# Three products of split fp32 weights: one accumulator and three 256-column matmuls in place of two halves and a join

## The chip, the cores and the metric

The kernel runs on one core of a Trainium2 chip. The metric is the device time of one execution in microseconds (us). Three runs of the kernel before gave 2520.5, 2520.75 and 2521.31 us, median 2520.75.

## The reference

A causal decoder trunk of two layers works on one sequence of 256 tokens with 2048 features, all in fp32. Each layer is

```
a = rmsnorm(h, attn_norm[i])
h = h + mixer(a)                                  # layer 0: stick-breaking and dilated heads; layer 1: forgetting attention
h = h + conv_ffn(rmsnorm(h, ffn_norm[i]))         # up projection to 2 x 5632, causal convolution of width 3,
                                                  # silu(gate) * value, down projection
h = h + sigmoid(rmsnorm(h, ple_norm[i]) @ w_ple_gate[i]) * (p[i] @ w_ple[i])
```

and a last rmsnorm follows. Nearly all of the arithmetic is in the products of activations with weights: q, k and v (2048 x 6144), the output projection (2048 x 2048), the up projection (2048 x 11264), the down projection (5632 x 2048) and the gate (2048 x 2048).

## The kernel before

**Products.** Every weight w and every activation a is kept as a sum of two fp32r parts, w = w0 + w1 and a = a0 + a1, and a product is w0 a0 + w0 a1 + w1 a0. The activations stand feature-major, 128 features to a partition, in tiles `act` of shape 128 x 16 x 2 x 256: for each of the 16 tiles k of features the two parts lie side by side, 256 tokens each. Two such tiles (X and Y in the code) take turns as input and output of the stages.

**Weight stream.** All weights come in one stream of pieces, in the order of their use. A piece holds up to 4 tiles k of 256 columns. `issue_group` (line 149) has SyncE bring pieces in transfers of up to 1 MB. `split_unit` makes the parts of a piece: ScalarE casts (line 165), VectorE subtracts (line 166), into one of four tiles `w`. Pieces are split up to three ahead of their use (`LOOK = 3`).

**Two matmuls for three products.** `gemm_unit` takes a piece and, for each half j of its 256 columns and each tile k, issues two matmuls into a result `ps[:, j]` of 512 columns of the accumulator memory (PSUM):

```
nc.tensor.matmul(ps[:, j], lhsT=w[:, k, 0, js], rhs=a, ...)                # line 207, 512 columns: w0 a0 | w0 a1
nc.tensor.matmul(ps[:, j, 1, :], lhsT=w[:, k, 1, js], rhs=a[:, 0, :], ...) # line 209, 256 columns: w1 a0 onto w0 a1
```

The result thus stands in two halves whose sum is wanted. `gemm_v` (lines 242 and 244) does the same for v with the activations as the stationary operand. A matmul is two instructions: the weight load (PEld in the profile) and the matmul (PE). `flat=True` (line 203), used for the products psp of the layer's own inputs p alone, issues three matmuls of 256 columns into one half; so do `gemm_vf` (line 256, 272 columns, the first v of layer 1 with its forget gates) and the last pair of gates (line 734, pse and psg).

**Joins.** `joined` has ScalarE copy one half of a result out (line 263) and VectorE add the other (line 264); the next step, for example the multiplication by the norm's reciprocal root `rb` (line 634), reads the sum. It serves psq, psk, psu and psg. `add_to_h` does the like for pso and psd (lines 270 to 272), and the end of `head_pair` for psv (lines 623 and 624).

**Accumulators.** The results of the projections come from `mm_tile`: 2 buffers of 2 x 512 columns each. Everything else (norm sums nps, rows rps, scores scs and sps, attention outputs avp) comes from `at_tile`, also 2 buffers of that size, as does psp of layer 1.

**Order.** The code of a layer is written in the order of its stages: 8 pairs of heads, each with psq, psk and psv of 4 pieces; then the 8 pairs of outputs of pso; then three blocks of the feed-forward network, each with its psu pieces and then psd; then 8 pairs psg of gates. Work of TensorE that waits for other engines is put off by some pieces: `defer(n, fn)` runs fn after n more pieces have been issued. So the small matmuls of attention and of the norm (nps at line 306, rps at line 339) stand within the rows of the projections. A scheduler then orders each engine's instructions by when it expects their inputs, so that nps and rps can stand in the middle of a piece.

Of the kernel before, what the change touches and what calls it, by code (L numbers as in the profile page):

```python
# [17 lines left out]
P = 128  # L18
D = 2048
S = 256  # L20
# [40 lines left out]
def _units():  # L61
    """Pieces of the weights, in the order in which they are used."""
    full = _cuts(KT)
    ple = [[("w_ple", l, 0, 2, c * 256, 256) for c in range(8)] for l in range(DEPTH)]
    out = list(ple[0])
    for l in range(DEPTH):
        for hp in range(NH // 2):
            if l % 2 == 1 and hp == 0:
                out += [("w_vf", l, k0, kc, 2 * D, 256 + NH) for k0, kc in VF_CUTS]
            for part in range(3):  # L70
                if l % 2 == 0 or hp > 0 or part < 2:
                    out += _pair("w_in", l, part * D + hp * 256, 0, full)
# [12 lines left out]

def _groups(units):
    """Pieces that one transfer brings."""
    out, i = [], 0
    while i < len(units):
        room = 512 if i < 2 else 1024 if i < 12 else 2048  # L90
        n, size = 0, 0
        while i + n < len(units) and size + units[i + n][3] * units[i + n][5] <= room:
            size += units[i + n][3] * units[i + n][5]
            n += 1
        out.append(units[i:i + n])
        i += n
    return out
# [7 lines left out]
def trunk(ctx: ExitStack, tc: tile.TileContext, xT, pT, pos, gains, conv, bf, cst, wst, out):  # L105
# [22 lines left out]
    def mm_tile(name):  # L128
        return psum.tile([P, 2, 2, S], F32, name=name, tag="mm", bufs=2)
# [49 lines left out]
    # what waits for other engines is given to TensorE some pieces later  # L179
# [14 lines left out]
    def gemm_unit(ps, act, kind, l, c0, k0, first, last, koff=0, flat=False):  # L194
        """ps[:, j, 0] and ps[:, j, 1] sum to W[:, 128 columns]^T A^T."""
        kc, w = unit(kind, l, k0, c0)
        for j in range(2):
            js = slice(j * P, (j + 1) * P)
            for k in range(kc):
                a = act[:, k0 - koff + k]  # L200
                if flat:
                    for n, (s, t) in enumerate(((0, 0), (0, 1), (1, 0))):
                        nc.tensor.matmul(ps[:, j, 0, :], lhsT=w[:, k, s, js], rhs=a[:, t, :],  # L203
                                         start=first and k == 0 and n == 0,
                                         stop=last and k == kc - 1 and n == 2)
                    continue
                nc.tensor.matmul(ps[:, j], lhsT=w[:, k, 0, js], rhs=a,  # L207
                                 start=first and k == 0, stop=False, skip_group_check=True)
                nc.tensor.matmul(ps[:, j, 1, :], lhsT=w[:, k, 1, js], rhs=a[:, 0, :],  # L209
                                 start=False, stop=last and k == kc - 1, skip_group_check=True)  # L210
        tick()

    def gemm(ps, act, kind, l, c0, cuts, k0=0, koff=0, part=None, flat=False):
        n = len(cuts)
        for i, kc in enumerate(cuts):
            if part is None or i in part:
                gemm_unit(ps, act, kind, l, c0, k0, i == 0, i == n - 1, koff, flat)
            k0 += kc

    def staggered(name, act, kind, l, cuts, done, k0=0, koff=0):  # L220
        """All pairs of outputs; the first two end together."""
        n = len(cuts)
        ps = [mm_tile(name) for _ in range(2)]
        for part in (range(n - 1), (n - 1,)):
            for op in range(2):
                gemm(ps[op], act, kind, l, op * 256, cuts, k0, koff, part)
                if part == (n - 1,):
                    done(op, ps[op])
        for op in range(2, 8):
            p = mm_tile(name)  # L230
            gemm(p, act, kind, l, op * 256, cuts, k0, koff)
            done(op, p)

    def gemm_v(ps, act, l, c0):
        """ps[:, t, 0] and ps[:, t, 1] sum to A[tokens of tile t] W[:, 256 columns]."""
        for i in range(4):
            kc, w = unit("w_in", l, 4 * i, c0)
            for t in range(2):
                tsl = slice(t * P, (t + 1) * P)
                for k in range(kc):  # L240
                    a = act[:, 4 * i + k]
                    nc.tensor.matmul(ps[:, t], lhsT=a[:, 0, tsl], rhs=w[:, k],  # L242
                                     start=i == 0 and k == 0, stop=False, skip_group_check=True)
# [17 lines left out]
    def joined(ps):  # L261
        t = t2_tile("jn")
        nc.scalar.copy(out=t, in_=ps[:, :, 1, :])  # L263
        nc.vector.tensor_add(out=t, in0=t, in1=ps[:, :, 0, :])  # L264
# [15 lines left out]
    def norm_parts(op, g, dst):  # L280
        """h pair op is final: its parts, with the gains."""
# [17 lines left out]
    def norm_sums(more=()):  # L299
        """Reciprocal roots of the mean squares, one token a partition."""  # L300
# [23 lines left out]
    def norm_rows(mixer):  # L324
        """The same, one token a column, in every partition."""
# [23 lines left out]
    def with_rows(fn):  # L349
        """fn reads rb: not before norm_rows."""  # L350
# [14 lines left out]
    def ple_up(l, op):  # L365
        """A pair of p W_ple, kept until its gates are there."""
        ps = at_tile("psp").rearrange("p j (a s) -> p j a s", a=2) if l > 0 else mm_tile("psp")
        gemm(ps, pact, "w_ple", l, op * 256, (2,), flat=True)
        nc.scalar.copy(out=pl[:, 2 * op:2 * op + 2, :], in_=ps[:, :, 0, :])
# [150 lines left out]
    def sm_second(pe, s):  # L520
        """The weights, one key a partition."""
# [60 lines left out]
    def head_pair(l, hp, act, dst, st):  # L582
# [4 lines left out]
        if l % 2 == 1 and hp == 0:  # L587
            ps = mm_tile("psv").rearrange("p t a s -> p t (a s)")
# [7 lines left out]
        with_rows(lambda ps=ps: nc.vector.tensor_mul(out=q, in0=joined(ps), in1=rq2))  # L596
# [24 lines left out]
        t = t2_tile("jv")  # L621
        for i in range(2):
            nc.scalar.activation(out=t[:, i, :], in_=ps[:, i, 1, :], func=AF.Copy, scale=rT[:, i:i + 1])
            nc.vector.scalar_tensor_tensor(out=v[:, i, :], in0=ps[:, i, 0, :], scalar=rT[:, i:i + 1],
                                           in1=t[:, i, :], op0=ALU.mult, op1=ALU.add)

    def ffn_group(l, g, g0, act, hid):
        c = [t2_tile("yg"), t2_tile("yv")]

        def conv_taps(half, ps):  # L630
# [3 lines left out]
            nc.vector.tensor_mul(out=u[:, :, 2:], in0=joined(ps), in1=rb2)  # L634
# [19 lines left out]
    X, Y = bufs  # L654
    for l in range(DEPTH):
# [51 lines left out]
        for op in range(8):  # L707
            end = l + 1 == DEPTH and op == 7
            if end:
                ws = [unit("w_ple_gate", l, 4 * i, op * 256)[1] for i in range(4)]  # L710
                ps = [at_tile("pse"), mm_tile("psg")[:, 0]]
# [4 lines left out]
            def gate(op, ps, hs):  # L716
                gt = joined(ps)
                nc.vector.tensor_mul(out=gt, in0=gt, in1=rb2)
# [10 lines left out]
            else:  # L729
                more = []  # L730
                for j in range(2):
                    for k in range(KT):
                        for n, (a, b) in enumerate(((0, 0), (0, 1), (1, 0))):
                            nc.tensor.matmul(ps[j][:, 0, :S],
# [5 lines left out]
                    nc.vector.tensor_mul(out=gt, in0=ps[j][:, 0, :S], in1=rb)  # L740
# [95 lines left out]
```

## Time and profile before

| | |
|---|---|
| median of three runs | 2520.75 us |
| span of the profiled execution | 2519.2 us |
| TensorE matmuls | 14270, busy 2497.2 us |
| TensorE weight loads | 14270, busy 2173.1 us |
| VectorE | 2386 instructions, busy 1716.3 us |
| ScalarE | 1747 instructions, busy 1319.4 us |
| moved by DMA | 457.20 MB, 181 GB/s on average |
| granted TensorE clock | full in every slice of the span |

The profiled execution has a span of its own, 1.5 us below the median of the runs. A matmul starts before the one ahead of it has ended, and the ends are modelled, so its duration (397 ns for 512 columns, 281 ns for 256) is longer than the distance to the next start. In the timeline the first column is the start and the second the duration in us, from the first start to the last end where rows are merged (xN). PE is the matmul, PEld the weight load, DVE VectorE, ACT ScalarE. A name such as psu<-act,w gives the tile written and the tiles read.

### The profile page before, as it was taken

What the parts mean: (1) busy time and instruction counts of PE and PEld (TensorE: products, weight loads), DVE (VectorE), ACT (ScalarE), POOL (GpSimd) and SP (SyncE); (2) the same over time, 40 slices, a digit from 0 to 9 for tenths busy, and PEclk for the clock granted to TensorE, in tenths of its full rate; (3) what the DMA queues carried; (4) which work ended last, traced back from release to release, by engine and by line L of the source; (5) the groups of instructions that cost most, each with busy time, mean ns of one, the idle gap of its engine ahead of it and who ended that gap; (6) DMA issues with size and microseconds to landing.
All of it is one profiled execution on the core that took longest, in us unless ns stands there. A gap on an engine that the chain in (4) does not pass through costs nothing. (4 is left out here: it accounts for less than half of the span.)

```text
span 2519.2 us, 34810 instructions
## 1 busy us (share of the span) xinstructions
PE 2497.2 (99%) x14270; PEld 2173.1 (86%) x14270; DVE 1716.3 (68%) x2386; ACT 1319.4 (52%) x1747; POOL 2.5 (0%) x8
## 2 busy tenths in 40 slices
PE   8999999999999999999999999999999999999997
PEld 7888888888888888888888888888888888888887
DVE  7767667776567657777765555677765776677676
ACT  6554455554455445555554444555544554455564
POOL 0000000000000000000000000000000000000000
PEclk9999999999999999999999999999999999999999
DMA  7444455555555555555454444555555555555553
GB/s 259 167 168 167 167 184 184 185 184 192 183 193 184 180 188 184 190 181 199 170 179 163 163 161 165 183 192 184 187 184 184 187 184 186 193 187 180 182 191 117
DMA packets 66431, 457.20 MB, mean 181 GB/s; under 512 B 7408, under 2 KB 7424, under 8 KB 16608
## 3 DMA queue, kind: packets, MB, share of 16 engines
q1 hardware_dynamic: 66096, 454.53, 50.5%
q8 instruction: 111, 1.82, 0.3%
q0 software_dynamic: 176, 0.46, 0.1%
q14 instruction: 48, 0.39, 0.0%
HBM read 452.86 MB, written 2.10 MB: 181 GB/s over the span
## 5 line engine op out<-in xcount | busy, mean ns | idle before, releaser
L166 DVE TENSOR_TENSOR w<-wr,w 128x1024 fp32r<-128x1024 f32 (+2 forms) x882 | 1049.8, 1191 | 532.3 <-ACT w L165 529.9
L165 ACT CAST w<-wr 128x1024 fp32r<-128x1024 f32 (+2 forms) x882 | 903.4, 1025 | 710.6 <-PE psd L209 186.7
L207 PE MATMUL psu<-act,w 128*128 128x512 f32 x2816 | 995.5, 397 | 0.0
L209 PE MATMUL psu<-act,w 128*128 128x256 f32 x2816 | 791.3, 281 | 0.0
L207 PEld LDWEIGHTS psu<-act,w 128*128 128x128 f32 x2816 | 529.4, 188 | 130.6
L209 PEld LDWEIGHTS psu<-act,w 128*128 128x128 f32 x2816 | 528.6, 188 | 0.0
L207 PE MATMUL psd<-act,w 128*128 128x512 f32 x1408 | 497.8, 397 | 0.0
L209 PE MATMUL psd<-act,w 128*128 128x256 f32 x1408 | 395.6, 281 | 0.0
L207 PEld LDWEIGHTS psd<-act,w 128*128 128x128 f32 x1408 | 264.7, 188 | 65.3
L209 PEld LDWEIGHTS psd<-act,w 128*128 128x128 f32 x1408 | 264.3, 188 | 0.0
L207 PE MATMUL psq<-act,w 128*128 128x512 f32 x512 | 183.9, 400 | 0.0
L207 PE MATMUL psk<-act,w 128*128 128x512 f32 x512 | 182.8, 399 | 0.0
L207 PE MATMUL pso<-act,w 128*128 128x512 f32 x512 | 181.5, 398 | 0.0
L242 PE MATMUL psv<-w,act 128*128 128x512 f32 x480 | 172.5, 399 | 0.7 <-DVE jn L264 0.7
L207 PE MATMUL psg<-act,w 128*128 128x512 f32 x480 | 170.0, 398 | 0.0
L209 PE MATMUL psq<-act,w 128*128 128x256 f32 x512 | 143.9, 281 | 0.7 <-DVE w L166 0.7
L209 PE MATMUL psk<-act,w 128*128 128x256 f32 x512 | 143.9, 281 | 0.0
L209 PE MATMUL pso<-act,w 128*128 128x256 f32 x512 | 143.9, 281 | 0.0
L244 PE MATMUL psv<-w,act 128*128 128x256 f32 x480 | 135.2, 282 | 0.0
L209 PE MATMUL psg<-act,w 128*128 128x256 f32 x480 | 134.9, 281 | 0.0
L263 ACT COPY jn<-psu 128x512 f32<-128x512 f32 x88 | 51.7, 588 | 147.0 <-PE psu L209 147.0
L264 DVE TENSOR_TENSOR jn<-jn,psu 128x512 f32<-128x512 f32 x88 | 60.5, 688 | 93.0 <-ACT jn L263 93.0
(202 smaller groups left out, 2317.0 us busy)
## 6 DMA issues: line engine op xcount, KB each, us to landing
wr<-in_w SPq DMA_DIRECT2D x388, 1024.0 KB, 4.8
wr<-in_w SPq DMA_DIRECT2D x36, 768.0 KB, 4.3
wr<-in_w SPq DMA_DIRECT2D x8, 896.0 KB, 4.6
wr<-in_w SPq DMA_DIRECT2D x7, 512.0 KB, 5.1
h<-in_x SPq DMA_DIRECT2D x4, 512.0 KB, 7.2
out_dram<-h SPq DMA_DIRECT2D x8, 256.0 KB, 2.4
wr<-in_w SPq DMA_DIRECT2D x2, 816.0 KB, 4.7
ct<-in_c SPq DMA_DIRECT2D x1, 841.0 KB, 6.6
```

What stands on the lines that cost most here:

```text
L165: nc.scalar.copy(out=w[:, :, 0, :], in_=raw)
L166: nc.vector.tensor_sub(out=w[:, :, 1, :], in0=raw, in1=w[:, :, 0, :].bitcast(F32))
L207: nc.tensor.matmul(ps[:, j], lhsT=w[:, k, 0, js], rhs=a, start=first and k == 0, stop=False, skip_group_check=True)
L209: nc.tensor.matmul(ps[:, j, 1, :], lhsT=w[:, k, 1, js], rhs=a[:, 0, :], start=False, stop=last and k == kc - 1, skip_group_check=True)
L242: nc.tensor.matmul(ps[:, t], lhsT=a[:, 0, tsl], rhs=w[:, k], start=i == 0 and k == 0, stop=False, skip_group_check=True)
L244: nc.tensor.matmul(ps[:, t, 1, :], lhsT=a[:, 1, tsl], rhs=w[:, k, 0, :], start=False, stop=i == 3 and k == kc - 1, skip_group_check=True)
L263: nc.scalar.copy(out=t, in_=ps[:, :, 1, :])
L264: nc.vector.tensor_add(out=t, in0=t, in1=ps[:, :, 0, :])
```

## The change

Every product is now made as `flat` made it: three matmuls of 256 columns, one after the other, into one accumulator of 256 columns. The results for j = 0 and j = 1 of a piece lie side by side in 512 columns. `mm_tile` has 4 buffers of that size in place of 2 of twice the size. The joins are gone: what read the joined sum reads the accumulator. psp of layer 1 moves from `at_tile` to `mm_tile`, and the first v of layer 1 with its forget gates from `mm_tile` to `at_tile`.

```
     def mm_tile(name):
-        return psum.tile([P, 2, 2, S], F32, name=name, tag="mm", bufs=2)
+        return psum.tile([P, 2, S], F32, name=name, tag="mm", bufs=4)
...
+    PARTS = ((0, 0), (0, 1), (1, 0))
...
             for k in range(kc):
-                a = act[:, k0 - koff + k]
...
-                nc.tensor.matmul(ps[:, j], lhsT=w[:, k, 0, js], rhs=a,
-                                 start=first and k == 0, stop=False, skip_group_check=True)
-                nc.tensor.matmul(ps[:, j, 1, :], lhsT=w[:, k, 1, js], rhs=a[:, 0, :],
-                                 start=False, stop=last and k == kc - 1, skip_group_check=True)
+                for n, (s, t) in enumerate(PARTS):
+                    nc.tensor.matmul(ps[:, j, :], lhsT=w[:, k, s, js], rhs=act[:, k0 - koff + k, t, :],
+                                     start=first and j + k + n == 0,
+                                     stop=last and k == kc - 1 and n == 2, skip_group_check=True)
...
-                    nc.tensor.matmul(ps[:, t], lhsT=a[:, 0, tsl], rhs=w[:, k],
-                                     start=i == 0 and k == 0, stop=False, skip_group_check=True)
-                    nc.tensor.matmul(ps[:, t, 1, :], lhsT=a[:, 1, tsl], rhs=w[:, k, 0, :],
-                                     start=False, stop=i == 3 and k == kc - 1, skip_group_check=True)
+                    for n, (a, b) in enumerate(PARTS):
+                        nc.tensor.matmul(ps[:, t], lhsT=act[:, 4 * i + k, a, tsl], rhs=w[:, k, b],
+                                         start=i + t + k + n == 0,
+                                         stop=i == 3 and k == kc - 1 and n == 2, skip_group_check=True)
...
-    def joined(ps):
-        t = t2_tile("jn")
-        nc.scalar.copy(out=t, in_=ps[:, :, 1, :])
-        nc.vector.tensor_add(out=t, in0=t, in1=ps[:, :, 0, :])
-        return t
-
     def add_to_h(op, ps):
         hs = h[:, 2 * op:2 * op + 2, :]
-        t = t2_tile("jh")
-        nc.scalar.copy(out=t, in_=ps[:, :, 1, :])
-        nc.vector.tensor_add(out=hs, in0=hs, in1=ps[:, :, 0, :])
-        nc.vector.tensor_add(out=hs, in0=hs, in1=t)
+        nc.vector.tensor_add(out=hs, in0=hs, in1=ps)
...
-        ps = at_tile("psp").rearrange("p j (a s) -> p j a s", a=2) if l > 0 else mm_tile("psp")
-        gemm(ps, pact, "w_ple", l, op * 256, (2,), flat=True)
+        ps = mm_tile("psp")
+        gemm(ps, pact, "w_ple", l, op * 256, (2,))
...
-            ps = mm_tile("psv").rearrange("p t a s -> p t (a s)")
+            ps = at_tile("psv")
...
-        nc.vector.tensor_mul(out=k, in0=joined(ps), in1=rb2)
+        nc.vector.tensor_mul(out=k, in0=ps, in1=rb2)
...
-        t = t2_tile("jv")
         for i in range(2):
-            nc.scalar.activation(out=t[:, i, :], in_=ps[:, i, 1, :], func=AF.Copy, scale=rT[:, i:i + 1])
-            nc.vector.scalar_tensor_tensor(out=v[:, i, :], in0=ps[:, i, 0, :], scalar=rT[:, i:i + 1],
-                                           in1=t[:, i, :], op0=ALU.mult, op1=ALU.add)
+            nc.scalar.activation(out=v[:, i, :], in_=ps[:, i, :], func=AF.Copy, scale=rT[:, i:i + 1])
...
-            nc.vector.tensor_mul(out=u[:, :, 2:], in0=joined(ps), in1=rb2)
+            nc.vector.tensor_mul(out=u[:, :, 2:], in0=ps, in1=rb2)
...
-                ps = [at_tile("pse"), mm_tile("psg")[:, 0]]
+                ps = [at_tile("pse")[:, j, :S] for j in range(2)]
...
-                gt = joined(ps)
-                nc.vector.tensor_mul(out=gt, in0=gt, in1=rb2)
+                gt = t2_tile("gt")
+                nc.vector.tensor_mul(out=gt, in0=ps, in1=rb2)
```

The change also moves instructions. Line 207 and its like of the kernel before are line 203 after, line 306 (nps) is line 291, and line 339 (rps) is line 324. On TensorE, at the start of the first feed-forward network, where the up projection psu is interrupted by the norm's sums nps and rows rps, there stood before

```order
L209 MATMUL psu<-act_68,w 128x256
L306 MATMUL nps<-ct,acc 128x2 x2
L207 MATMUL psu<-act_68,w 128x512
L209 MATMUL psu<-act_68,w 128x256
L207 MATMUL psu<-act_68,w 128x512
...
L209 MATMUL psu<-act_68,w 128x256
L339 MATMUL rps<-ndh,trir 128x256
L339 MATMUL rps<-ndl,trir 128x256
L207 MATMUL psu<-act_68,w 128x512
```

and now

```order
L203 MATMUL pso<-act_69,w 128x256 x648
L203 MATMUL psu<-act_68,w 128x256 x72
L291 MATMUL nps<-ct,acc 128x2 x2
L203 MATMUL psu<-act_68,w 128x256 x48
L324 MATMUL rps<-ndh,trir 128x256
L324 MATMUL rps<-ndl,trir 128x256
L203 MATMUL psu<-act_68,w 128x256 x1416
L203 MATMUL psd<-act_69,w 128x256 x768
```

The 16 pairs between nps and rps became 48 matmuls of one form, and the rows of the up and the down projection that follow are unbroken rows of that form.

Also on TensorE, at the start of layer 1, where v and the forget gates (psv, 272 columns) are projected together and the norm of the layer's input is not yet known, there stood before

```order
L256 MATMUL psv<-w,act_69 128x272 x63
L306 MATMUL nps<-ct,acc 128x2 x2
L256 MATMUL psv<-w,act_69 128x272 x33
L207 MATMUL psq<-act_69,w 128x512
...
L207 MATMUL psq<-act_69,w 128x512
L339 MATMUL rps<-ndh,trir 128x256
L209 MATMUL psq<-act_69,w 128x256
```

and now

```order
L250 MATMUL psv<-w,act_69 128x272 x54
L291 MATMUL nps<-ct,acc 128x2 x2
L250 MATMUL psv<-w,act_69 128x272 x33
L324 MATMUL rps<-ndh,trir 128x256
L250 MATMUL psv<-w,act_69 128x272 x8
L324 MATMUL rps<-ndl,trir 128x256
L250 MATMUL psv<-w,act_69 128x272
L203 MATMUL psq<-act_69,w 128x256 x72
```

The two rps matmuls moved from behind the thirteenth matmul of psq and later, after the end of psv, to within the last nine matmuls of psv.

On ScalarE, in the first pair of heads, there stood before

```order
L336 CAST ndh<-nd 128x256
L165 CAST w<-wr 128x4x256
L263 COPY jn<-psq 128x512
L263 COPY jn<-psk 128x512
L165 CAST w<-wr 128x4x256 x4
L454 ACTIVATE e<-e 128x768
```

and now

```order
L321 CAST ndh<-nd 128x256
L165 CAST w<-wr 128x4x256 x5
L439 ACTIVATE e<-e 128x768
L411 ACT_TABLE_LOAD
L411 ACTIVATE rs<-ang,ct 32x256
```

The two copies of the join (jn) are gone from between the casts of weight pieces.

More of the change, by code (lines that the diff above doesn't have):

```diff
@@ L192, in tick, with gemm_unit @@
             due[0][1]()
-    def gemm_unit(ps, act, kind, l, c0, k0, first, last, koff=0, flat=False):
+    PARTS = ((0, 0), (0, 1), (1, 0))
+    def gemm_unit(ps, act, kind, l, c0, k0, first, last, koff=0):
         kc, w = unit(kind, l, k0, c0)
@@ L199, in gemm_unit, with gemm @@
             for k in range(kc):
-                a = act[:, k0 - koff + k]
[L201 to L207, printed above, removed]
-                                 start=first and k == 0, stop=False, skip_group_check=True)
-                nc.tensor.matmul(ps[:, j, 1, :], lhsT=w[:, k, 1, js], rhs=a[:, 0, :],
-                                 start=False, stop=last and k == kc - 1, skip_group_check=True)
+                for n, (s, t) in enumerate(PARTS):
+                    nc.tensor.matmul(ps[:, j, :], lhsT=w[:, k, s, js], rhs=act[:, k0 - koff + k, t, :],
+                                     start=first and j + k + n == 0,
+                                     stop=last and k == kc - 1 and n == 2, skip_group_check=True)
         tick()
-    def gemm(ps, act, kind, l, c0, cuts, k0=0, koff=0, part=None, flat=False):
+    def gemm(ps, act, kind, l, c0, cuts, k0=0, koff=0, part=None):
         n = len(cuts)
@@ L216, in gemm @@
             if part is None or i in part:
-                gemm_unit(ps, act, kind, l, c0, k0, i == 0, i == n - 1, koff, flat)
+                gemm_unit(ps, act, kind, l, c0, k0, i == 0, i == n - 1, koff)
             k0 += kc
@@ L240, in gemm_v @@
                 for k in range(kc):
-                    a = act[:, 4 * i + k]
-                    nc.tensor.matmul(ps[:, t], lhsT=a[:, 0, tsl], rhs=w[:, k],
-                                     start=i == 0 and k == 0, stop=False, skip_group_check=True)
-                    nc.tensor.matmul(ps[:, t, 1, :], lhsT=a[:, 1, tsl], rhs=w[:, k, 0, :],
-                                     start=False, stop=i == 3 and k == kc - 1, skip_group_check=True)
+                    for n, (a, b) in enumerate(PARTS):
+                        nc.tensor.matmul(ps[:, t], lhsT=act[:, 4 * i + k, a, tsl], rhs=w[:, k, b],
+                                         start=i + t + k + n == 0,
+                                         stop=i == 3 and k == kc - 1 and n == 2, skip_group_check=True)
             tick()
@@ L365, in ple_up @@
     def ple_up(l, op):
-        ps = at_tile("psp").rearrange("p j (a s) -> p j a s", a=2) if l > 0 else mm_tile("psp")
-        gemm(ps, pact, "w_ple", l, op * 256, (2,), flat=True)
-        nc.scalar.copy(out=pl[:, 2 * op:2 * op + 2, :], in_=ps[:, :, 0, :])
+        ps = mm_tile("psp")
+        gemm(ps, pact, "w_ple", l, op * 256, (2,))
+        nc.scalar.copy(out=pl[:, 2 * op:2 * op + 2, :], in_=ps)
     def load_x(i):
@@ L595, in head_pair @@
         gemm(ps, act, "w_in", l, hp * 256, full)
-        with_rows(lambda ps=ps: nc.vector.tensor_mul(out=q, in0=joined(ps), in1=rq2))
+        with_rows(lambda ps=ps: nc.vector.tensor_mul(out=q, in0=ps, in1=rq2))
         ps = mm_tile("psk")
         gemm(ps, act, "w_in", l, D + hp * 256, full)
-        nc.vector.tensor_mul(out=k, in0=joined(ps), in1=rb2)
+        nc.vector.tensor_mul(out=k, in0=ps, in1=rb2)
         def first():
@@ L733, in trunk @@
                         for n, (a, b) in enumerate(((0, 0), (0, 1), (1, 0))):
-                            nc.tensor.matmul(ps[j][:, 0, :S],
+                            nc.tensor.matmul(ps[j],
                                              lhsT=ws[k // 4][:, k % 4, a, j * P:(j + 1) * P],
@@ L739, in trunk @@
                     hj = h[:, 2 * op + j, :]
-                    nc.vector.tensor_mul(out=gt, in0=ps[j][:, 0, :S], in1=rb)
+                    nc.vector.tensor_mul(out=gt, in0=ps[j], in1=rb)
                     nc.scalar.activation(out=gt, in_=gt, func=AF.Sigmoid)
```

## Prediction

> **What bounds the kernel now.** I read the page first, then the waits of TensorE, then its timeline row by row in several places, and the windows of those places last.
>
> ```profile
> span 2519.2 us, 34810 instructions
> PE 2497.2 (99%) x14270; PEld 2173.1 (86%) x14270; DVE 1716.3 (68%) x2386; ACT 1319.4 (52%) x1747; POOL 2.5 (0%) x8
> PE 49%; DVE 0%; DVEq 0%; issue 0%; ACT 0%
> ```
>
> TensorE is busy for 99% of the span and the chain that ended last runs on nothing else. VectorE and ScalarE have 32% and 48% of the span to spare. The view of TensorE's own waits shows how little it waits for them:
>
> ```profile
> PE psp L203 <- ACT w L165: 5.9, 2, 5.4
> PE rps L331 <- DVE nd L329: 2.7, 1, 2.7
> PE nps L306 <- DVE sq L745: 1.6, 1, 1.6
> PE psp L203 <- ACT pl L369: 1.4, 2, 1.3
> PE psq L209 <- DVE w L166: 0.7, 1, 0.7
> PE psv L242 <- DVE jn L264: 0.7, 1, 0.7
> ```
>
> All six lines sum to 13.0 us, and only the last one and the one on pl have to do with what the change touches. So the time is the pace of TensorE: so many matmuls, each so long after the one before. Durations overlap, so starts are what I compare. In the middle of the first layer's up projection:
>
> ```profile
> 1002.30 0.40 PE L207 MATMUL psu<-act,w 128*128 128x512 f32 x1
> ...
> 1011.84 0.40 PE L207 MATMUL psu<-act,w 128*128 128x512 f32 x1
> ```
>
> Between these starts lie 27 pairs of a 512-column and a 256-column matmul: 9.54 / 27 = 353 ns for each k tile and 128 outputs. This pair is what the change replaces.
>
> **The change, part by part: the matmuls.** The groups of the pairs are
>
> ```profile
> L207 PE MATMUL psu<-act,w 128*128 128x512 f32 x2816 | 995.5, 397 | 0.0
> L207 PE MATMUL psd<-act,w 128*128 128x512 f32 x1408 | 497.8, 397 | 0.0
> L207 PE MATMUL psq<-act,w 128*128 128x512 f32 x512 | 183.9, 400 | 0.0
> L242 PE MATMUL psv<-w,act 128*128 128x512 f32 x480 | 172.5, 399 | 0.7 <-DVE jn L264 0.7
> ```
>
> with psk and pso of the count of psq, and psg of that of psv: 2816 + 1408 + 3 x 512 + 2 x 480 = 6720 pairs. At 353.3 ns they are 2374 us, 94% of the span. Afterwards they are 20160 matmuls of 256 columns, each with its own weight load. The columns are the same (768 per pair), so everything hangs on what one 256-column matmul in an unbroken row of its like costs. The kernel before has such rows: psp, pse and the last psg already run the three products into one accumulator, and psv of line 256 does it with 272 columns.
>
> ```profile
> 16.80 2.43 PE L203 MATMUL psp<-pact,w 128*128 128x256 f32 x20
> 1332.74 1.53 PE L203 MATMUL psp<-pact,w 128*128 128x256 f32 x12
> 1334.11 0.39 PE L207 MATMUL psq<-act,w 128*128 128x512 f32 x1
> 1290.37 1.58 PE L203 MATMUL psp<-pact,w 128*128 128x256 f32 x12
> 1291.78 0.40 PE L207 MATMUL psq<-act,w 128*128 128x512 f32 x1
> 1252.82 8.02 PE L256 MATMUL psv<-w,act 128*128 128x272 f32 x63
> 2492.04 5.82 PE L734 MATMUL pse<-act,w 128*128 128x256 f32 x48
> 2497.70 5.82 PE L734 MATMUL psg<-act,w 128*128 128x256 f32 x48
> ```
>
> They show two paces. The 48 of pse take 5.66 us from start to start, 117.9 ns each, or 353.7 for three: the price of today's pair to 0.4 ns. The psp row at 1290.37 gives 1.41 / 12 = 117.5, and the 272 columns of psv give (8.02 - 0.29) / 62 = 124.7, which is 117.4 per 256. But the 20 of psp at 16.80 take (2.43 - 0.28) / 19 = 113.2, and those at 1332.74 take 1.37 / 12 = 114.2 with the first one slow. So the same instruction has a slow pace of 117.8 and a fast one of 113.3, 4.5 ns apart, and 20160 x 4.5 = 91 us hang on which one the new rows take.
>
> What decides it? The windows (columns: span, PE busy with count, granted clock, DMA share, GB/s) exclude two suspects:
>
> ```profile
> 16.50:21.00 4.50, 4.50 (x42) 1.00 0.95 348
> 1332.80:1334.00 1.20, 1.20 (x13) 1.00 0.00 0
> 2492.10:2497.60 5.50, 5.50 (x49) 1.00 0.00 0
> ```
>
> The granted clock is 1.00 in all, and the fast pace is there with DMA at 0.95 and at 0.00, the slow one at 0.00. What does go with it is what ran just ahead. Both slow rows of 256 columns follow the 512/256 alternation at once (psk ahead of 1290.37, psg ahead of 2492.04) and keep its pace. The fast ones follow a wait, or the projections of v, whose spacing varies. And the alternation itself is faster for a moment when it has been interrupted, here after the four small nps matmuls at 423.2, with an activation tile as the moving operand:
>
> ```profile
> 423.99 0.39 PE L207 MATMUL psu<-act,w 128*128 128x512 f32 x1
> ...
> 424.33 0.39 PE L207 MATMUL psu<-act,w 128*128 128x512 f32 x1
> ...
> 424.68 0.39 PE L207 MATMUL psu<-act,w 128*128 128x512 f32 x1
> ...
> 425.02 0.40 PE L207 MATMUL psu<-act,w 128*128 128x512 f32 x1
> 425.26 0.28 PE L209 MATMUL psu<-act,w 128*128 128x256 f32 x1
> 425.38 0.40 PE L207 MATMUL psu<-act,w 128*128 128x512 f32 x1
> ```
>
> Three pairs take 1.03 us, 343 each, and then 360 and on at 353. I read this as two rhythms of TensorE's read and load, where the alternation always falls back into the slow one and an even row keeps the one that it enters. In the changed kernel the alternation is gone: the program enters with the fast psp, and from there on each interruption (nps, rps, scores, sps, avp) starts a row anew. It is an inference from few rows, and none shows a row of more than some 60 at the fast pace; hence the wide range.
>
> The Trainium skill ("TensorE: Matmul & The Clock Gate", section "Back-to-back issue gap") gives a warm gap of N / 2.4 + 2.5 ns, a fixed 2.5 per matmul; by it three matmuls cost 2.5 ns more than the pair, and the sum would be 6720 x 2.5 = 17 us slower, an estimate from that page. The trace disagrees with its sizes: 117.9 and 353 stand where the formula has 109 and 325.
>
> **Weight loads.** Each new matmul brings one. In pse they take
>
> ```profile
> L734 PEld LDWEIGHTS pse<-act,w x48: 187/188/192, 2491.9 to 2497.5; 128*128 128x128 f32 x48
> ```
>
> 188 ns at a spacing of 117.9, so loads overlap one another and 188 is no floor. 6720 more of them cost nothing of their own as long as a matmul of 256 columns hides one; the 113.3 of psp contains one as well.
>
> **The joins.** Gone are, per result, a copy on ScalarE and an addition on VectorE:
>
> ```profile
> L263 ACT COPY jn<-psu 128x512 f32<-128x512 f32 x88 | 51.7, 588 | 147.0 <-PE psu L209 147.0
> L264 DVE TENSOR_TENSOR jn<-jn,psu 128x512 f32<-128x512 f32 x88 | 60.5, 688 | 93.0 <-ACT jn L263 93.0
> ```
>
> Besides the 88 of psu there are 47 of q, k and the gate and 64 of the residual, where the second addition goes: 199 x 0.588 = 117 us of ScalarE and 199 x 0.688 = 137 us of VectorE, which also loses 30 short additions of v. All of it lies beside TensorE's matmuls; on the path it is worth nothing but the two waits on pl and jn, 2.1 us. Four result buffers in place of two cover the same waits. Were TensorE's cover gone, these sums are the most that they could be worth. At the fast pace VectorE has some (1716 - 137) / 2435 = 65% of the span to work, so it does not become the bound.
>
> **Order.** In the forget-gate projection rps moves from the middle of psq to 33 matmuls after nps. Before,
>
> ```profile
> 1260.89 0.61 PE L306 MATMUL nps<-ct,acc 128*128 128x2 f32 x4
> 1267.76 0.41 ACT L336 CAST ndh<-nd 128x256 fp32r<-128x256 f32 x1
> ```
>
> ndh is ready 6.8 us after nps began to be read (1261.4 to 1268.2); 33 x 0.125 = 4.1 us of matmuls cover only part. TensorE then waits 0 to 2.7 us, and behind it stand the last 9 of that projection and psq. I take 2: it cancels the 2.1 gained.
>
> **Sum.** The stretches that few things interrupt (psu, psd, pso, psg) hold 3 x (2816 + 1408 + 512 + 480) = 15648 matmuls, the attention projections 4512. I take the fast pace for the first and for two thirds of the second, as often interrupted rows sometimes land on the slow one: (15648 + 3008) x 4.5 = 84 us. 2519 - 84 = 2435 for the span; the median of the runs, 2520.75, is 1.5 us above the profiled span, and some rows will enter slowly, so I write 2440.
>
> **The rivals.** *Slow pace kept.* The rows fall into 117.8 as pse and psg did for 96 matmuls: 353.7 for 353.3 is at most +3 us (the rows are given to 0.01 us), the waits -2, rps +2: 2521 to 2524, no change. For it: the only long rows with the activation tile and nothing interrupting them are slow. Against it: both entered from the alternation.
> *Half and half.* One layer's feed-forward stretch lands fast and the other slow. One of them is 4224 + 2112 = 6336 matmuls, 29 us; with the pso and psg rows and the projections mixed, about 2480.
> *Slower: TensorE is fed too slowly.* Place: the long psu and psd rows. Today an instruction (load or matmul) is due every 353 / 4 = 88 ns, then every 57 to 59. The rows of pse show that pace for 96 matmuls only, which instructions issued ahead of time could hide. Should the feed give 120 ns a matmul, the 20160 cost 20160 x 2.2 = 44 us, 2565; it decides from 118.1 ns on (5 us). For it: no row of this kind is longer. Against it: the second 48 at the end take the same 5.82 us as the first.
> *Slower: a fixed cost of each matmul.* One more matmul for each of the 6720 pairs; the rows of pse put it at 0.4 ns, which stays within no change, and from 0.75 ns on it is 5 us. At 1.5 ns, four times what the rows show, it is 10 us, 2531.
> *Loads as the bound.* A rule of the Trainium skill ("Perfetto Trace Analysis", "Identifying the Most-Contended Engine") judges TensorE's headroom by the busy share of the weight loads. Worked out from rows: 2173 us of loads + 6720 x 0.188 = 3436 us, more than the span; if loads could not overlap, that would be the time. The pse row rules it out, 48 x 188 = 9.0 us of loads in 5.7; I give it no chance above 1 in 100.
>
> **How the numbers follow.** Fast pace in most rows 0.45; half and half 0.17; slow pace kept 0.26; slower 0.12 (the feed 0.07, a fixed cost 0.04, loads 0.01). Differences below 0.2%, 5 us, can't be told from no change. Faster 0.62, the same 0.26, slower 0.12. The range goes from all rows fast, 2521 - 91 - 2 = 2428, to the unchanged pace with every small loss, 2524; the likeliest case's own range is 2428 to 2462.
>
> **What would show it.** In the profile after: starts in the long rows 113.3 apart (right), 117.8 (the first rival), over 118 (the feed); both paces in different stretches for the half; TensorE's waits still some 13 us; VectorE and ScalarE down by some 140 and 117 us with no effect on the span. I am wrong if the rows of psu and psd do not run at 113 to 114 ns.

## The result and the profile after

The changed kernel takes 2437.77 us (median of 4 runs, 2437.26 to 2438.14) beside 2520.62 us of the kernel before (4 runs, 2520.17 to 2521.31): a ratio of 0.967, 95% interval 0.966 to 0.968, 83 us faster. The forecast was 2440 us.

The page of the changed kernel, in the lines that answer to those of before (its run took 2438.14 us, of which the span is 2436.3):

```profile
span 2436.3 us, 48002 instructions
PE 2414.1 (99%) x20990; PEld 2400.5 (99%) x20990; DVE 1595.7 (65%) x2157; ACT 1228.3 (50%) x1548; POOL 2.5 (0%) x8
...
L203 PE MATMUL psu<-act,w 128*128 128x256 f32 x8448 | 959.3, 276 | 0.0
L203 PEld LDWEIGHTS psu<-act,w 128*128 128x128 f32 x8448 | 958.3, 188 | 0.0
L203 PE MATMUL psd<-act,w 128*128 128x256 f32 x4224 | 479.7, 276 | 0.0
```

TensorE is as full as before (99%). Its busy time fell by 2497.2 - 2414.1 = 83.1 us and the span by 82.9: all of the gain is TensorE's pace. In the group rows the busy time counts overlapped time once, so busy time by count is close to the spacing of an unbroken row: 959.3 / 8448 = 113.6 ns for psu, 479.7 / 4224 = 113.6 for psd (276 is how long one lasts).

The same stretch in the middle of the first up projection, 500 us long, by the windows of both kernels (columns: stretch, its length, then busy time with count of PE, PEld, DVE, ACT and POOL, granted clock, DMA share, GB/s). Before:

```profile
500.00:1000.00 500.00, 500.00 (x2832) 434.26 (x2831) 337.03 (x447) 254.32 (x314) 0.00 (x0) 1.00 0.52 187
```

and after:

```profile
500.00:1000.00 500.00, 500.00 (x4415) 500.00 (x4413) 326.42 (x422) 244.44 (x282) 0.00 (x0) 1.00 0.55 194
```

2832 matmuls are 1416 pairs, 353.11 ns each; 4415 are 1471.7 triples, 339.75 ns each, or 113.25 for a matmul. The granted clock is 1.00 in both. Such a window holds some 4400 matmuls at the fast pace. The longest fast row of before, the psp row of which the prediction shows 20, has 35 at that pace in its trace. The waits of TensorE, after:

```profile
PE psp L203 <- ACT w L165: 6.1, 3, 5.6
PE rps L316 <- DVE nd L314: 2.7, 1, 2.7
PE nps L291 <- DVE sq L727: 1.6, 1, 1.6
PE rps L324 <- ACT ndh L321: 1.0, 2, 0.9
PE psq L203 <- DVE w L166: 1.0, 1, 1.0
PE psp L203 <- DVE w L166: 0.5, 2, 0.2
PE nps L291 <- DVE acc L287: 0.4, 1, 0.4
```

They sum to 13.3 us, beside 13.0 before. The waits on pl and jn (2.1 us) are gone; the one of rps on ndh (1.0 us) is new.

Not every row is fast. In the first layer, behind the scores of the fifth pair of heads, the timeline (columns: start, length, engine, line, instruction, count):

```profile
203.76 0.60 PE L469 MATMUL scs<-k,q 128*128 128x256 f32 x2
204.01 3.18 PE L237 MATMUL psv<-w,act 128*128 128x256 f32 x24
207.02 8.65 PE L203 MATMUL psq<-act,w 128*128 128x256 f32 x72
215.51 0.82 PE L511 MATMUL sps<-ct,pe 128*128 128x128 f32 x6
216.08 2.98 PE L203 MATMUL psq<-act,w 128*128 128x256 f32 x24
218.90 2.88 PE L203 MATMUL psk<-act,w 128*128 128x256 f32 x24
```

Behind the scores (scs) the 72 of psq run at (8.65 - 0.28) / 71 = 117.9 ns; behind sps the 24 of psk run at (2.88 - 0.28) / 23 = 113.0. The two paces of the forecast are both there, and here an interruption lies between them.

### The profile page after: what moved, and what is told of

It reads as the page before. It is cut to its first block, busy times and chain, and to the rows that moved or that the text cites. A ratio compares the mean times of both kernels' runs of the same rounds, so it can differ in the third digit from the quotient of the medians.

```text
span 2436.3 us, 48002 instructions
## 1 busy us (share of the span) xinstructions
PE 2414.1 (99%) x20990; PEld 2400.5 (99%) x20990; DVE 1595.7 (65%) x2157; ACT 1228.3 (50%) x1548; POOL 2.5 (0%) x8
## 4 chain that ended last, share of the span: by engine, by line
PE 97%; DVE 1%; DMA 1%; ACT 1%; issue 0%; SPq 0%; DVEq 0%; ACTq 0%
PE psu L203 39%; PE psd L203 20%; PE pso L203 7%; PE psk L203 7%; PE psv L237 7%; PE psq L203 7%; PE psg L203 7%; DMA wr<-in_w 1%; PE avp L520 1%; PE psp L203 0%; PE pse L716 0%; PE scs L469 0%; PE psv L250 0%; PE sps L511 0%; PE avp L522 0%; PE scs L467 0%
## 5 line engine op out<-in xcount | busy, mean ns | idle before, releaser
L203 PE MATMUL psu<-act,w 128*128 128x256 f32 x8448 | 959.3, 276 | 0.0
L203 PEld LDWEIGHTS psu<-act,w 128*128 128x128 f32 x8448 | 958.3, 188 | 0.0
L203 PE MATMUL psd<-act,w 128*128 128x256 f32 x4224 | 479.7, 276 | 0.0
L203 PEld LDWEIGHTS psq<-act,w 128*128 128x128 f32 x1536 | 179.8, 188 | 2.1 <-DVE w L166 1.5
L203 PEld LDWEIGHTS psk<-act,w 128*128 128x128 f32 x1536 | 176.7, 188 | 0.0
L203 PEld LDWEIGHTS pso<-act,w 128*128 128x128 f32 x1536 | 174.9, 188 | 0.0
L237 PEld LDWEIGHTS psv<-w,act 128*128 128x128 f32 x1440 | 168.4, 188 | 1.1
L203 PEld LDWEIGHTS psg<-act,w 128*128 128x128 f32 x1440 | 163.7, 188 | 0.0
L622 DVE SCALAR_TENSOR_TENSOR yg<-u,cv,yg 128x256 f32<-128x256 f32 x176 | 73.3, 477 | 0.0
L622 DVE SCALAR_TENSOR_TENSOR yv<-u,cv,yv 128x256 f32<-128x256 f32 x176 | 73.3, 477 | 0.0
```

What stands on the lines that cost most here:

```text
L203: nc.tensor.matmul(ps[:, j, :], lhsT=w[:, k, s, js], rhs=act[:, k0 - koff + k, t, :], start=first and j + k + n == 0, stop=last and k == k ...
L237: nc.tensor.matmul(ps[:, t], lhsT=act[:, 4 * i + k, a, tsl], rhs=w[:, k, b], start=i + t + k + n == 0, stop=i == 3 and k == kc - 1 and n = ...
L622: nc.vector.scalar_tensor_tensor(out=y[:, j, :], in0=u[:, j, tap:tap + S], scalar=cv[:, l, t, tap:tap + 1], in1=y[:, j, :], op0=ALU.mult, ...
```

## The experiments

Two theories stood against each other at first. P: the gain is TensorE's pace, since an even row of 256-column matmuls can hold a rhythm that the alternation of 512 and 256 columns can't. R: the gain comes from the joins that are gone. A third one, about where the operands lie in SBUF, came later. The kernel before was run again beside each group of kernels and took 2521.56 us beside the first four, 2522.68 beside the next four, 2521.84 beside the next three and 2522.11 beside the last. Ratios are to these, with a 95% interval.

### Three matmuls, joins kept

```
-    nc.tensor.matmul(ps[:, j], lhsT=w[:, k, 0, js], rhs=a, ...)
-    nc.tensor.matmul(ps[:, j, 1, :], lhsT=w[:, k, 1, js], rhs=a[:, 0, :], ...)
+    for n, (s, t) in enumerate(((0, 0), (0, 1), (1, 0))):
+        nc.tensor.matmul(ps[:, j, min(n, 1), :], lhsT=w[:, k, s, js], rhs=a[:, t, :], ...)
```

> The kernel before, with the products made by three 256-column matmuls (first product into one half, the other two into the other), and with both halves, their buffers and all joins kept. Theory P (TensorE's pace: an even row of 256-column matmuls runs at 113.3 ns, the 512/256 alternation at 353 ns a pair): 2436 to 2446 us, psu starts 113.3 ns apart. Rival R (the gain came from the joins that went: less work of VectorE and ScalarE, less traffic at the accumulators): 2515 to 2521 us.

Measured: 2438.01 us (2437.07 to 2439.52), 0.967 (0.966 to 0.969), the time of the changed kernel. Its page shows the joins still at work:

```profile
PE 2415.6 (99%) x20990; PEld 2402.5 (99%) x20990; DVE 1714.6 (70%) x2386; ACT 1323.7 (54%) x1747; POOL 2.5 (0%) x8
...
L263 ACT COPY jn<-psu 128x512 f32<-128x512 f32 x88 | 51.6, 587 | 140.3 <-PE psu L208 140.3
```

VectorE and ScalarE are as loaded as in the kernel before (1716.3 and 1319.4), and the whole gain is there. The matmuls alone bring it.

### Pairs, no joins

```
     def joined(ps):
-        t = t2_tile("jn")
-        nc.scalar.copy(out=t, in_=ps[:, :, 1, :])
-        nc.vector.tensor_add(out=t, in0=t, in1=ps[:, :, 0, :])
-        return t
+        return ps[:, :, 0, :]
```

and likewise for v and the residual. This kernel leaves the second half out of every result.

> The kernel before with its 512/256 pairs, but with the joins left out: the readers take the first half alone, so the two small products are left out of every result. Theory P: 2517 to 2521 us, psu pairs still 353 ns apart. Rival R: 2436 to 2446 us.

Measured: 2522.27 us (2520.90 to 2523.96), 1.0004 (0.9995 to 1.0013).

```profile
PE 2497.2 (99%) x14270; PEld 2173.4 (86%) x14270; DVE 1595.5 (63%) x2157; ACT 1222.3 (48%) x1548; POOL 2.5 (0%) x8
```

VectorE and ScalarE have the load of the changed kernel, TensorE the busy time of the kernel before to 0.1 us, and nothing is gained. R falls on both sides.

### One alternating result in a kernel of threes

In the changed kernel the first half of the third group of the up projection (g == 2) is made with pairs and a join again, once in each layer: 32 pairs in each, 64 out of 6720.

```
+    alt = g == 2 and half == 0
+    ps = at_tile("psx").rearrange(...) if alt else mm_tile("psu")
```

> The changed kernel, but one result of psu near the start of each layer's feed-forward stretch (the gate half of group 2) is made by 512/256 pairs and joined; the 5760 matmuls behind it in each layer's psu and psd are untouched. Theory P with memory (an even row keeps the pace that it enters): the rows behind the alternating result run at 117.8 ns until the next small matmuls of the norm, 2 x (5760 + 72) x 4.5 = 52 us and 1 us for the pairs, 2488 to 2493 us. Rival M (no memory, the form alone sets the pace): 2438 to 2441 us, psu and psd at 113.3 ns but for some matmuls.

Measured: 2490.78 us (2490.45 to 2491.76), 0.988 (0.987 to 0.990), as theory P with memory had it. 64 pairs cost 53 us. The windows of TensorE alone, ahead of the alternating result, behind it, much later, and behind the next norm:

```profile
428.00:448.00 20.00, 20.00 (x179) 1.00 0.50 177
462.00:482.00 20.00, 20.00 (x172) 1.00 0.48 168
500.00:1000.00 500.00, 500.00 (x4247) 1.00 0.52 186
1165.00:1200.00 35.00, 35.00 (x311) 1.00 0.55 192
```

Ahead of it 179 matmuls fit in 20 us, behind it 172, and the 500 us window holds 4247 in place of 4415, 117.7 ns each. These are the same instructions in the same code: the rows behind the alternating result keep for some 700 us the pace that they entered with. At 1165, behind nps and rps of the next norm, it is the fast one again (a count includes the two or three that a window's edges cut, so 311 in 35 us are about 113.4 ns).

### Eight of 512, then eight of 256

The kernel before, joins kept, but in each piece all 512-column matmuls first, then all 256-column ones (v as before).

> The kernel before with joins, in which each piece issues its eight 512-column matmuls first and then its eight 256-column ones (v stays in alternation). If it is the alternation that holds the slow pace: groups of eight settle at 113.3 and twice that, 340 ns a pair, 2440 to 2460 us. If any mix of the two sizes holds it: 353 ns a pair, 2515 to 2521 us. If the 512-column form alone is slow: 235 + 113.3 = 348, 2480 to 2495 us.

Measured: 2481.66 us (2479.51 to 2482.27), 0.984 (0.983 to 0.986), about half of the gain, with the instructions of the kernel before. The time is that of the third expectation, a slow form of 512 columns, and outside the other two. The timeline in the up projection, and the window:

```profile
1002.05 1.07 PE L214 MATMUL psu<-act,w 128*128 128x256 f32 x8
1002.97 2.02 PE L210 MATMUL psu<-act,w 128*128 128x512 f32 x8
1004.83 1.07 PE L214 MATMUL psu<-act,w 128*128 128x256 f32 x8
```

```profile
500.00:1000.00 500.00, 500.00 (x2889) 1.00 0.53 190
```

The 256-column ones take (1.07 - 0.28) / 7 = 113 ns, the 512-column ones (2.02 - 0.40) / 7 = 231 rather than 2 x 113.3 = 227. In the window a pair takes 500 / 1444.5 = 346.1 ns in place of 353.1. So the order of the forms is worth 7.0 of the 13.4 ns that separate a pair from three matmuls of 256; the rest is in the 512-column form, which doesn't reach the fast pace in full, and in the changes of form that remain.

### Where the operands lie: first a test of another explanation

The forecast took two rhythms of TensorE's read and load as given. If it is these two, where the operands lie in SBUF should matter. In the built program the activations begin at byte 32896 of a partition and the first weight piece at 163008; the distance, 130112 = 254 x 512 + 64, is 64 above a multiple of 512. The other buffers and k tiles of both lie whole multiples of 1024 bytes from these, and the second 128 outputs of a piece 512 bytes on, so the distance modulo 512 is 64 for every load of the long rows and the columns that it meets. The accumulators lie at the same places in all of the kernels that follow. A pad ahead of the weight pool moves the pieces (posi, which now shares the bytes of rs, makes room, and moves them down by 1024; rc and rs are made a few lines earlier for it):

```
+    wpool.tile([P, 16], F32, name="pad", tag="pad")
-    posi = cpool.tile([32, S], I32, name="posi")
+    posi = rs.bitcast(I32)
```

So the move is by 960 bytes down, not by the 64 bytes that the first two expectations say; the distance modulo 512 becomes 128, as meant. The kernel before, with it:

> The kernel before, with every weight piece (w) and raw piece (wr) moved by 64 bytes in SBUF, so that weight pieces and activations both start at a multiple of 128 bytes; before, the weight pieces start 64 bytes off. Theory A (the 117.8 ns rhythm comes from how the rows read for a load lie against those read for the matmul): pairs fall from 353 to about 340 ns, 2436 to 2450 us. Theory P (the rhythm belongs to the alternation of 512 and 256 columns, wherever the tiles lie): pairs stay at 353 ns, 2519 to 2524 us.

Measured: 2509.19 us (2508.77 to 2509.55), 0.995 (0.993 to 0.996). And the changed kernel:

> The changed kernel with the same move by 64 bytes. Theory A: the stretches of 117.8 ns that remain behind scs (about 1290 matmuls x 4.45 ns = 5.7 us) go, 2431 to 2434 us; or, if the moved place is the bad one, all rows slow, 2515 to 2525 us. Theory P: nothing changes, 2437 to 2439 us.

Measured: 2538.19 us (2538.16 to 2540.28), 1.006 (1.005 to 1.008). The same window of the two, pairs first:

```profile
500.00:1000.00 500.00, 500.00 (x2850) 1.00 0.52 188
```

```profile
500.00:1000.00 500.00, 500.00 (x4216) 1.00 0.52 185
```

Pairs take 500 / 1425 = 350.9 ns, a matmul of the threes 118.6. Neither theory's times were met, by either kernel: the place matters, to both, and in opposite directions. At this place the very change of this study is 2538.19 - 2509.19 = 29 us slower.

### Does a short matmul let go of the slow pace?

The kernel with one alternating result, with two matmuls of 128 columns behind that result:

```
+    kp = at_tile("kps")
+    for t in range(2):
+        nc.tensor.matmul(kp[:, 0, t * P:(t + 1) * P], lhsT=ones, rhs=ident, ...)
```

> The kernel e3_one_alternating_result (2490.8 us) with two matmuls of 128 columns (ones by the identity, into a bank of their own that nobody reads) put behind each of the two results that are made with 512 and 256 columns. Theory P with memory (an even row keeps the pace that it enters with, and a short matmul of another form lets the next row enter afresh): the rows behind go back to 113.3 ns, only the 64 pairs stay slow (64 x 13 ns = 0.8 us) and the added matmuls cost under 1 us: 2437.5 to 2442 us. If the short matmuls don't let go of the slow pace, or the rows of e3 are slow for another reason than the pace they entered with: 2489 to 2493 us.

Measured: 2492.05 us (2491.61 to 2493.82), 0.988 (0.987 to 0.989): it doesn't. Each added matmul shows as two in the trace.

```profile
460.02 0.60 PE L646 MATMUL kps<-ct 128*128 128x128 f32 x4
460.38 5.78 PE L210 MATMUL psu<-act,w 128*128 128x256 f32 x47
```

Behind the short ones the row takes some 200 ns for its first step and then 117.8: (5.78 - 0.28 - 0.20) / 45. The changed kernel with one such matmul behind each group of scores:

```
+    nc.tensor.matmul(sc[:, 1, 384:512], lhsT=ones, rhs=ident, start=False, stop=True, ...)
```

> The changed kernel with one matmul of 128 columns (ones by the identity, into columns of the scs bank that nobody reads) put behind each of the 16 groups of scs matmuls, where the trace of the changed kernel shows the next projection rows at 117.8 ns. Theory P with memory: those rows (about 1190 x 4.45 ns = 5.3 us) go to 113.3 ns, less 16 added matmuls at 0.11 to 0.22 us (1.8 to 3.5 us): 2434 to 2436.5 us. If the entry behind scs is slow for another reason: 2439 to 2441.5 us.

Measured: 2438.90 us (2438.74 to 2439.55), 0.967 (0.966 to 0.968), no better than the changed kernel, and 0.1 us below the range for "another reason". Two places in the second layer:

```profile
1283.59 0.49 PE L480 MATMUL scs<-ct 128*128 128x128 f32 x2
1283.83 5.69 PE L237 MATMUL psv<-w,act 128*128 128x256 f32 x48
1289.36 1.58 PE L203 MATMUL psp<-pact,w 128*128 128x256 f32 x12
...
1439.47 0.49 PE L480 MATMUL scs<-ct 128*128 128x128 f32 x2
1439.72 5.55 PE L237 MATMUL psv<-w,act 128*128 128x256 f32 x45
...
1445.45 1.53 PE L203 MATMUL psp<-pact,w 128*128 128x256 f32 x12
```

At 1283.83 the row holds 113.4 (5.53 us to the next start, less 0.20 for the first step, over 47), at 1439.72 it holds 117.9 ((5.55 - 0.28 - 0.20) / 43), behind the same instructions. So an interruption gives the row a new chance, and no sure outcome; which pace comes out is not told by the form that went ahead. The pace can also change without a small matmul in between, where v's product ends, the one in which activations are loaded and weights move: the psp row behind the fast psv is slow, (1.58 - 0.28) / 11 = 118 ns, and the one behind the slow psv fast, (1.53 - 0.28) / 11 = 114. Counted row by row in the two traces, 718 matmuls stand in slow rows in place of 1258; these 540 are worth 540 x 4.45 = 2.4 us, and the 16 added matmuls, at the 0.24 us that the rows above show, cost some 3.8. That leaves 1.4 us of loss, where the two medians differ by 1.1.

### The distance between weights and activations

> The changed kernel with the weight pieces 896 bytes lower in SBUF: again 64 bytes off a multiple of 128, as in the changed kernel itself; activations where they were. (In e5 and e6 they lay 960 bytes lower, at a multiple of 128: a pad of 64 bytes, less 1024 that were saved elsewhere.) Theory L (the place of the weight pieces modulo 128 against the activations sets which rhythm the rows can hold): rows at 113.3 ns again, 2437 to 2439.5 us. If it is the move itself, or the place in a larger raster: rows between 114 and 119 ns, 2445 to 2545 us.

> The changed kernel with the weight pieces 992 bytes lower: 96 bytes above a multiple of 128, half-way between the place of the changed kernel (64) and that of e6 (0). Theory L gives no value by itself: if every place off the multiple of 128 does as 64 does, 2437 to 2439.5 us; if only the place 64 does, and the others are as in e6, 2530 to 2545 us; below 2436 us the place is better than either.

> The changed kernel with activations 64 bytes higher and weight pieces 960 bytes lower, as in e6: now the activations lie 64 bytes off a multiple of 128 and the weight pieces at one, so the difference between the two modulo 128 is 64 again. If the difference of the two places counts: 2437 to 2439.5 us. If the place of the weight pieces alone counts: 2530 to 2545 us as in e6.

> The changed kernel with the weight pieces 64 bytes lower, so that their distance to the activations is a multiple of 1024 bytes (a load and the columns that it meets start at the same place of every raster up to 1024). What the runs have shown of the distance modulo 256: 64 (the changed kernel; e11, where both moved): rows at 113.3 ns, 2437 to 2438 us; 192 (e9): both rhythms, mostly 117.8 ns, 2510 us; 128 (e6): 115 to 122 ns, 2538 us; 96 (e10): about 118 ns, 2521 to 2548 us. Theory D (the distance sets the rhythm): this is one more distance, with a time of its own; 2436 to 2440 us if 0 lets the rows hold 113.3 ns as 64 does, 2520 to 2545 us if it does as 96 and 128, under 2432 us if the rows hold 113.3 ns behind scs too. If neither place nor distance counts but each build falls by chance into a rhythm: any of these, and rows that change pace within a kernel without an interruption.

All four are the changed kernel with another pad: 32 words ahead of the weight pool, 8 words there, 16 words ahead of the activations, and 240 words ahead of the weight pool. Their psu groups, in this order:

```profile
L204 PE MATMUL psu<-act,w 128*128 128x256 f32 x8448 | 996.8, 279 | 0.0
```

```profile
L204 PE MATMUL psu<-act,w 128*128 128x256 f32 x8448 | 998.8, 280 | 0.0
```

```profile
L204 PE MATMUL psu<-act,w 128*128 128x256 f32 x8448 | 959.3, 276 | 0.0
```

```profile
L204 PE MATMUL psu<-act,w 128*128 128x256 f32 x8448 | 1015.5, 283 | 0.0
```

With the two from above (959.3 for the changed kernel, 1004.3 for the one moved to 128):

| distance modulo 512 | kernel of threes | psu, busy / count | time, us | ratio to before |
|---|---|---|---|---|
| 0 | weights 64 bytes lower | 120.2 ns | 2564.39 (2563.51 to 2565.33) | 1.017 (1.016 to 1.018) |
| 64 | as changed | 113.6 | 2437.77 (2437.26 to 2438.14) | 0.967 (0.966 to 0.968) |
| 64 | weights 960 lower, activations 64 higher | 113.6 | 2437.16 (2436.04 to 2438.09) | 0.966 (0.965 to 0.968) |
| 96 | weights 992 lower | 118.2 | 2529.62 (2520.79 to 2548.06) | 1.004 (1.001 to 1.007) |
| 128 | weights 960 lower | 118.9 | 2538.19 (2538.16 to 2540.28) | 1.006 (1.005 to 1.008) |
| 192 | weights 896 lower | 118.0 | 2510.00 (2509.04 to 2514.09) | 0.995 (0.993 to 0.997) |

The second row of 64 shows that neither place alone decides: its weights lie where those of the 2538 us kernel lie, and 64 bytes on the side of the activations bring all 101 us back, as expected if the difference counts. What it shares with the changed kernel is the distance, and with it the paces: counted row by row, every tile has as many matmuls in fast and in slow rows in the one trace as in the other (936 and 504 of psq, 816 and 624 of psv). The two builds agree to 0.6 us. That each build falls by chance into a rhythm has little for it here; the other distances were built once each.

The row of 192, which is 64 modulo 128, missed the time that Theory L gave it. But it runs at the same two paces as 64. Its long rows stand at the slow one, 500 / 4248 = 117.7 ns, and a psk row of the first layer at the fast one, (3.45 - 0.28) / 28 = 113.2:

```profile
500.00:1000.00 500.00, 500.00 (x4248) 1.00 0.52 187
```

```profile
225.78 3.45 PE L204 MATMUL psk<-act,w 128*128 128x256 f32 x29
```

So in these runs the distance sets which paces a row can have, and not by itself which of them it takes. A raster of 128 bytes falls with 0 and 128: both are multiples of 128, and their long rows take 120.0 and 118.6 ns. The raster is at least 256 bytes; how large it is was not tried. Distance 0 is the slowest of all, above every range that was expected of it.

At 96 the executions themselves differ by 27 us: four of the ten took 2520.8 to 2521.7 us, three 2529.0 to 2530.5 and three 2546.4 to 2548.1. The median of the ten lies 0.4 us below the range expected if only the place 64 is fast. The same window in the first layer and one like it in the second hold two paces in the profiled execution (2530.22 us), 500 / 4216 = 118.6 and 500 / 4263 = 117.3 ns:

```profile
500.00:1000.00 500.00, 500.00 (x4216) 1.00 0.51 185
1700.00:2200.00 500.00, 500.00 (x4263) 1.00 0.52 187
```

Over the 6336 matmuls of psu and psd in a layer these 1.3 ns are 8 us (an estimate from the two windows), about the step from the first group of executions to the second. So it seems that there the same program takes one pace or another from execution to execution; no trace of the other two groups was kept. With this, and with five distances, the table is not a rule.

The kernel at distance 0 shows that no other engine is needed for it. First the last 59 matmuls of pse in the changed kernel, at distance 64, with a window within them, then the last 51 at distance 0:

```profile
2413.79 6.85 PE L716 MATMUL pse<-act,w 128*128 128x256 f32 x59
```

```profile
2417.00:2420.00 3.00, 3.00 (x29) 3.00 (x28) 0.46 (x2) 0.51 (x1) 0.00 (x0) 1.00 0.00 0
```

```profile
2539.76 6.28 PE L716 MATMUL pse<-act,w 128*128 128x256 f32 x51
```

```profile
2542.00:2545.50 3.50, 3.50 (x31) 3.50 (x30) 0.54 (x2) 0.51 (x1) 0.00 (x0) 1.00 0.00 0
```

At distance 0 the spacing is (6.28 - 0.28) / 50 = 120.0 ns, as in the long rows, with VectorE at work for 0.54 us of 3.5, ScalarE for 0.51, no DMA, and the clock at 1.00. At 64 it is (6.85 - 0.28) / 58 = 113.3, with VectorE and ScalarE about as little at work (0.46 and 0.51 us of 3). What is left are the two things that TensorE itself reads there, the weights that it loads and the columns that it multiplies. That their reads get in each other's way is my reading of it; no view shows the reads.

None of the twelve kernels beats the changed one by more than the measurement tells: the best, 2437.16 us, has a range that overlaps its range.

## Why the prediction was right, and where its reasons fell short

**TensorE's pace carries the time.** Right: 83.1 us of its busy time for 82.9 us of span, and the two kernels that part the matmuls from the joins put all of it on the matmuls.

**113.3 ns in the long rows, 84 us in all.** Right in size and place. By the windows a triple gains 353.11 - 339.75 = 13.36 ns, which on the 5216 of psu, psd, pso and psg is 69.7 us. That leaves 13.2 us for the 1504 in the attention projections, which would be 20.1 if all were fast: 66%, where the forecast took two thirds. That every long row entered at the fast pace is in part luck: no row of before could show it, the forecast gave it 0.45, and at distance 192, with the same two paces to choose from, all long rows entered at the slow one.

**"The alternation always falls back into the slow one and an even row keeps the one that it enters."** Right at this distance, and for longer than I would have said: 32 alternating pairs slowed the 700 us of each layer that stand behind them. The words behind it, that each interruption "starts a row anew", were too simple. Two short matmuls left the slow pace standing, equal interruptions were followed by either pace, and the pace also changed where v's product ended, with no interruption.

**"I read this as two rhythms of TensorE's read and load."** This is the step that was too narrow. The two paces are not properties of the instruction. They belong to the distance of 64 bytes that this kernel happens to have (192 has them too): at 0 there is one pace, 120.0; at 128 the long rows run at 118.6, at 96 at 118.6 and 117.3; and at 128 the pairs are cheaper (350.9 ns) and the change loses 29 us. The forecast came out because the psp rows that gave 113.2 lie at the same distance as the new rows (pact is 65536 bytes from the activations). A rival from the operands' place was not among mine, and no row of the profile before could have priced it.

**Slow pace kept; half and half.** The first didn't happen in the long rows, but such mixtures do occur: the kernel of threes with one alternating result, at 2490.78 us, is nearly the half of the forecast (2480), and distance 192 gives 2510.

**The feed, a fixed cost, loads as the bound.** Not seen. TensorE was fed an instruction every 113.25 / 2 = 57 ns for 500 us on end. Loads are busy for 99% of the span, at 188 ns each, and also at distance 0, where they take 192 and the whole 5% longer: that share tells neither headroom nor pace.

**The joins.** Worth nothing, as said. Their sizes were a little off: VectorE's busy time fell by 120.6 us and ScalarE's by 91.1, where the sums had 137 and 117. Busy time counts overlapping instructions once. Added up one by one in the two traces, the instructions of VectorE fell by 150.0 us (the 137, and 14 for the additions of v) and those of ScalarE by 114.0.

**The order of rps.** The wait on ndh is 1.0 us where I took 2, and the sum of all waits rose by 0.3.

## What to carry to other kernels

When TensorE is full, look at the spacing of its starts, not at durations or busy shares, and ask whether equal instructions run at two spacings: here 4 to 7 ns of 113, which no wait and no clock shows, were worth 83 us between two forms of the products and 127 between two places of the weights. An even row of one form can hold a rhythm that a mixed one breaks, and one mixed result can spoil thousands of matmuls behind it. Before believing such a gain, or giving up on it, move one operand by some tens of bytes and measure again: the same kernel but for a pad was 3.3% faster or 1.7% slower than before by where its weights lay.

## What the runs showed of the hardware that was not expected

- The spacing of a 256-column matmul with its own load depends on the distance in bytes between the loaded weights and the moving columns: 113.3 ns at 64 (modulo 512), 118.6 at 128, 120.0 at 0, with the same instructions and clock; each load lasts 192 ns at 0 and 188 at the others. The Trainium skill ("SBUF — State Buffer", section "SBUF: two separate sides") says that within the engine side only the port shared by VectorE and GpSimd causes contention, and that PE never waits on anyone. The pse row above, with the other engines nearly idle, doesn't contradict that PE waits on no other engine, but shows that PE alone is not free of such an effect.
- At distance 64 two paces, 113.3 and 117.8 ns, can both last for hundreds of microseconds, and which one a row has depends on what ran before it.
- At distance 96 executions of one program range over 1.1% (2520.79 to 2548.06 us), at distances 64 and 128 over 0.1%. In its profile the long rows of the two layers run at two paces, 118.6 and 117.3 ns.
